# Identity products ahead of the first projections, and the decay tables behind a copy of the first head's queries

## The chip, the cores and the metric

The kernel runs on one core of a Trainium2 chip. A core has a matrix engine (TensorE, PE in the profile), a vector engine (VectorE, DVE), an engine for functions of one argument (ScalarE, ACT), a general engine (GpSimd, POOL) and SyncE (SP), which issues the transfers here. They share an on-chip memory of 128 partitions; TensorE writes into eight banks of PSUM, which VectorE and ScalarE empty. The metric is the device time of one execution, in microseconds, lower being better.

## The reference

The program is a small generator backbone of two layers over 256 latent tokens with a prefix of 256 context tokens, of width 1024. Layer 0 mixes tokens with bidirectional retention in four heads, layer 1 with neighbourhood attention; each is followed by a SwiGLU channel mixer. Every sublayer is modulated by the condition (adaLN; `modulate` is h * (1 + scale) + shift). What matters here is the beginning of layer 0:

```python
cond_lat = jax.nn.silu(c)[:, None, :]
cond_ctx = jax.nn.silu(c_ctx)[None, None, :]
m_lat = jnp.split(cond_lat @ ada_w[i] + ada_b[i], 6, axis=-1)
m_ctx = jnp.split(cond_ctx @ ada_w[i] + ada_b[i], 6, axis=-1)
a_lat = modulate(h_lat, m_lat[0], m_lat[1])
...
q, k, v, g = jnp.split(a @ w_in, [hk, 2 * hk, 2 * hk + hv], axis=-1)
log_gamma = -jnp.exp(decay_param.astype(jnp.float32))
o_ctx, o_lat = bidirectional_scan(ctx_terms, lat_terms)
y = rms_norm(o).transpose(0, 2, 1, 3).reshape(B, n, hv).astype(g.dtype)
return (jax.nn.silu(g) * y) @ w_out
```

The kernel computes the scan as one product of masked scores: for each head, the scores of keys against queries are multiplied by a table of powers of that head's decay and then multiplied with the values.

## The kernel before, in words

Tokens number 512, latents first. Weights arrive from HBM as units of 128 x 1024 floats, in the order of their use. A unit is split into a high half, a rounded copy made by ScalarE (line 124), and a low half, a subtraction on VectorE (line 126); three products (`mm3`, lines 144 to 146) then stand for one product of full precision. A unit takes one of three `raw` buffers while it is loaded and split.

The start of the kernel is a region whose order on every engine is written out by hand (`tc.manual_schedule`). It loads the condition, the adaLN weights and x. `spread_cond` (lines 174 to 184) spreads the context's condition over the partitions: for each of eight columns two products of that column, repeated 128 times, with the identity `identr`; two copies on ScalarE follow. Then a loop runs over eight K tiles of 128 input features. For each, VectorE sums four columns of the modulation (line 229), ScalarE modulates the x of this tile (line 412) and makes its high half (line 417), and TensorE adds the tile's products into eight banks: four of head 0's queries and keys (`qk0_0` to `qk0_3`) and four of its values. The first five K tiles multiply unsplit floats (`whole_products`, lines 355 and 358); for the last three, weights and activations are split (`split_products`, lines 363 to 373, with `low`, line 347, on VectorE). All eight banks are full when the region ends.

Behind the region, the instructions of each engine are put in order when the program is compiled: a planner goes by the order of the program, which is the priority, and by its own estimate of when each instruction would be ready. `tc.issue_after(ins)` adds to this that what is traced in the block stands behind `ins` in the queue of the engine of `ins`; work for other engines is not bound.

`decay_prep` and `decay_table` (lines 441 to 472) make one table for each head, in the order 1, 2, 3, 0. A table takes four exponentials on ScalarE (lines 461 and 466) and three products or sums on GpSimd (lines 462, 463 and 467). One buffer (`Dt`) holds the table; those of heads 1 to 3 are stored to HBM (line 469) and loaded again later, that of head 0 stays. Two scratch tiles of each table use the tag `pf`, which has two buffers. The same tag serves, later in the program, the eight half rows of x that are loaded and scaled into the residual `z` (lines 803 to 810, on GpSimd), and the scores of a head times their table (lines 558 and 562 on VectorE).

`qk_evac` (line 484) empties the banks of queries or keys: VectorE multiplies the latents by the rotary tables (line 492), ScalarE copies the context columns (line 497 from the first bank, line 500 from the second), VectorE combines them, and a split follows (lines 153 and 154). `v_evac` splits the four value banks. After these, TensorE goes on with head 0's gate (`proj_g`, tiles `g`), whose first bank is the one that `qk0_0` leaves, then head 0's scores (`S`), head 1's queries and keys, head 0's values (`O`), and so on.

Of the kernel before, what the change touches and what calls it, by code (L numbers as in the profile page):

```python
# [11 lines left out]
AF = mybir.ActivationFunctionType  # L12
# [6 lines left out]
P = 128  # L19
D = 1024  # L20
KT = D // P
NLAT = 256
# [22 lines left out]
def backbone(ctx: ExitStack, tc: tile.TileContext, wpack, adapack, cond, condcol, xT, xtok, adab, lncol, lnrow,  # L45
             decay, delta, rope, rpb, mask8, out):
    nc = tc.nc
# [31 lines left out]
    def bank(name):  # L79
        return psum.tile([P, 512], F32, tag="bank", name=name)  # L80
# [61 lines left out]
    def mm3(o, s, m, start, stop):  # L142

        nc.tensor.matmul(o, s[0], m[0], start=start, stop=False)  # L144
        nc.tensor.matmul(o, s[0], m[1], start=False, stop=False)  # L145
        nc.tensor.matmul(o, s[1], m[0], start=False, stop=stop)  # L146

    def cut(pair, *idx):
        return pair[0][idx], pair[1][idx]

    def split_into(pair, src, lo_eng=None, src2=None):

        return (nc.scalar.copy(pair[0], src),
                (lo_eng or nc.vector).tensor_tensor(out=pair[1], in0=src, in1=pair[0].bitcast(F32), op=ALU.subtract))
# [19 lines left out]
    def spread_cond():  # L174
        nc.vector.tensor_copy(out=chi, in_=ccol)
        nc.vector.tensor_tensor(out=clo, in0=ccol, in1=chi.bitcast(F32), op=ALU.subtract)
        for half in range(2):
            b = bank(f"cond_{half}")
            for i in range(4):
                k = 4 * half + i  # L180
                for n, c in enumerate((chi, clo)):
                    nc.tensor.matmul(b[:, i * P:i * P + P], c[:, k:k + 1].to_broadcast([P, P]), identr,
                                     start=i == 0 and n == 0, stop=i == 3 and n == 1)
            nc.scalar.copy(condb[1][:, half * 512:half * 512 + 512], b)
# [79 lines left out]
    identr = const.tile([P, P], F32R, name="identr")  # L264
# [56 lines left out]
    with Phase("ret", "yTh", "yTl", "vh", "vl", "kh", "kl") as rp:  # L321
# [12 lines left out]
                                      name=f"adaraw{i}")  # L334
        xts = {}
        lasts = []

        def load_x(kt):
            xts[kt] = rp.tile([P, NTOK], F32, tag=f"yT{'hl'[kt % 2]}{kt // 2 % 2}", name=f"xt{kt}")
            nc.sync.dma_start(xts[kt], xT[kt])  # L340
# [43 lines left out]
            stream.place[16 * RET_H - 4 + i] = (rp, w + "h", w + "l", 1)  # L384
        load_x(0)
        stream.load_to(1)
        spread_cond()
        qk_ps = [bank(f"qk0_{f}") for f in range(4)]
        v_ps = [bank(f"v0_{t}") for t in range(4)]
        for kt in range(KT):  # L390
# [50 lines left out]
        def decay_prep():  # L441
            nc.scalar.activation(lg, lg, AF.Exp)
            nc.gpsimd.tensor_scalar(out=lg, in0=lg, scalar1=-1.0, scalar2=0.0, op0=ALU.mult, op1=ALU.add)
            nc.gpsimd.tensor_scalar(out=lgw[:, 0], in0=lg, scalar1=256.0, scalar2=0.0, op0=ALU.mult, op1=ALU.add)
            nc.gpsimd.tensor_scalar(out=lgw[:, 1], in0=lg, scalar1=-1.0, scalar2=0.0, op0=ALU.mult, op1=ALU.add)
            nc.scalar.activation(dp[0], dlt, AF.Relu)
            nc.scalar.activation(dp[1], dlt, AF.Relu, scale=-1.0)

            nc.gpsimd.memset(dp[2], 1.0)
            nc.gpsimd.affine_select(out=dp[2], in_=dp[2], compare_op=ALU.not_equal, fill=2.0, base=-128,  # L450
                                    pattern=[[1, 384]], channel_multiplier=-1)
# [5 lines left out]
        def decay_table(h):  # L457
            D_ = rp.tile([P, 2, 384], F32, tag="Dt", name=f"Dw{h}")
            e = [rp.tile([P, 384], F32, tag=f"yT{'hl'[i]}3", name=f"de{i}_{h}") for i in range(2)]
            for i in range(2):  # L460
                nc.scalar.activation(e[i], dp[i], AF.Exp, scale=lg[:, 4 * i + h:4 * i + h + 1])
            nc.gpsimd.tensor_tensor(out=e[0], in0=e[0], in1=e[1], op=ALU.mult)
            nc.gpsimd.tensor_tensor(out=D_[:, 1, :], in0=e[0], in1=dp[2], op=ALU.mult)
            x = [rp.tile([P, NTOK], F32, tag="pf", name=f"dx{i}_{h}", bufs=2)[:, 0:384] for i in range(2)]
            for i, rate in enumerate((lg[:, h:h + 1], lgw[:, 1, 4 + h:5 + h])):
                nc.scalar.activation(x[i], dlt, AF.Exp, scale=rate, bias=lgw[:, 0, 4 * i + h:4 * i + h + 1])
            nc.gpsimd.tensor_tensor(out=D_[:, 0, :], in0=x[0], in1=x[1], op=ALU.add)
            if h:
                nc.sync.dma_start(dscr[h], D_)
            else:  # L470
                Dt[h] = D_

        with tc.issue_after(lasts[-1].ins):
            decay_prep()
            for h in (1, 2, 3, 0):
                decay_table(h)

        qk = {}
        vv = {}
        gg = {}  # L480
# [3 lines left out]
        def qk_evac(h, which, ps):  # L484

            f = rp.tile([P, 2, NTOK], F32, tag="qf", name=f"qf{h}{which}", bufs=1)
            scale = 1.0 / 16.0 if which == "q" else 1.0
            m = [rp.tile([P, NLAT], F32, tag=f"rm{i}", name=f"rm{i}_{h}{which}") for i in range(2)]
            x = [f[:, i, 0:NLAT] for i in range(2)]

            def times(o, i, table):
                nc.vector.scalar_tensor_tensor(out=o, in0=ps[i][:, 0:NLAT], scalar=scale, in1=table, op0=ALU.mult,
                                               op1=ALU.mult)

            times(x[0], 0, cosT)
            times(m[1], 0, sinT)
            nc.scalar.activation(f[:, 0, NLAT:], ps[0][:, NLAT:], AF.Copy, scale=scale)  # L497
            times(x[1], 1, cosT)
            times(m[0], 1, sinT)
            nc.scalar.activation(f[:, 1, NLAT:], ps[1][:, NLAT:], AF.Copy, scale=scale)  # L500
            nc.vector.tensor_tensor(out=x[0], in0=x[0], in1=m[0], op=ALU.subtract)
            nc.vector.tensor_tensor(out=x[1], in0=m[1], in1=x[1], op=ALU.add)
            pr = (rp.tile([P, 2, NTOK], F32R, tag=f"{which}h", name=f"{which}h{h}"),
                  rp.tile([P, 2, NTOK], F32R, tag=f"{which}l", name=f"{which}l{h}"))
            split_into(pr, f)
            qk[(h, which)] = pr

        def v_evac(h, ps):
            for t in CTX_FIRST:
                pr = (rp.tile([P, 512], F32R, tag=f"vh{t}", name=f"vh{t}_{h}"),  # L510
                      rp.tile([P, 512], F32R, tag=f"vl{t}", name=f"vl{t}_{h}"))
                split_into(pr, ps[t])
                vv[(h, t)] = pr

        def proj_qk(h):
            for which in "qk":
                ps = []
                for i in range(2):
                    u = stream.next()
                    b = bank(f"{which}{h}_{i}")  # L520
                    for kt in range(KT):
                        mm3(b, cut(u, slice(None), slice(kt * P, kt * P + P)), aT[kt], kt == 0, kt == KT - 1)
                    ps.append(b)
                qk_evac(h, which, ps)
# [12 lines left out]
        def proj_g(h):  # L537
            for i in range(4):
                u = stream.next()
                b = bank(f"g{h}_{i}")  # L540
                for kt in range(KT):
                    mm3(b, cut(u, slice(None), slice(kt * P, kt * P + P)), aT[kt], kt == 0, kt == KT - 1)
                g = rp.tile([P, NTOK], F32, tag=f"g{i}", name=f"g{i}_{h}")
                nc.scalar.activation(g, b, AF.Silu)
                gg[(h, i)] = g
# [254 lines left out]
        for i, w in ((0, "q"), (2, "k")):  # L800
            qk_evac(0, w, qk_ps[i:i + 2])
        v_evac(0, v_ps)
        proj_g(0)
        for t in CTX_FIRST:
            for half in range(2):
# [405 lines left out]
    with Phase("ffn1", "h1h", "h1l") as fp:  # L1211
# [62 lines left out]
        ps = {(t, c): bank(f"e_{t}{c}") for t in range(2) for c, _ in cols[t]}  # L1274
# [138 lines left out]
```

## Time and profile before

| | us |
|---|---|
| median of three runs (lowest, highest) | 1187.77 (1181.21, 1190.56) |
| the profiled execution, its own time | 1184.83 |
| its span, first to last instruction | 1182.8 |
| TensorE busy | 1155.5 (98%) |
| VectorE busy | 786.8 (67%) |
| ScalarE busy | 454.3 (38%) |
| GpSimd busy | 295.5 (25%) |

A line of the profile's timeline gives the start and the length in microseconds, the engine (`PEld` is the loading of TensorE's stationary operand, `SPq` an issue of a transfer), the line of the kernel, the operation, the tile written and the tiles read, and in square brackets the idle time of the engine before it and what ended that. `x8` merges eight instructions. A line of the waits gives who waited for whom, the total, how many times and the longest. A line of the windows gives a stretch and its length, then the busy time and the count of instructions of PE, PEld, DVE, ACT and POOL, the granted clock of TensorE as a share of the full one, the busy share of the transfer engines, and GB/s. A line of a source gives the least, the median and the longest duration in nanoseconds, and the first and last start. Operations that a helper issues all carry the helper's line.

### The profile page before, as it was taken

To read this page: it belongs to the slowest core of one execution; us is meant where nothing else is said; L and a number is where in the kernel's file an instruction comes from. 1 tells how busy PE (TensorE), PEld (TensorE's weight loads), DVE (VectorE), ACT (ScalarE), POOL (GpSimd) and SP (SyncE) were. 2 spreads that over 40 slices of the span, in tenths; PEclk is the share of its full clock that TensorE was granted. 3 is DMA by queue.
4 is the path that set the end of the run, shared out by engine and by line. 5 is a ranking of instruction groups with operands and counts; after the bars stand their busy time and mean duration, and the time that the engine had idled before them with its cause. 6 is when DMAs were issued, how large, how long until landed. Compare 5 with 4: busy or idle time off the path is not lost.

```text
span 1182.8 us, 15310 instructions
## 1 busy us (share of the span) xinstructions
PE 1155.5 (98%) x5670; PEld 961.8 (81%) x5670; DVE 786.8 (67%) x1136; ACT 454.3 (38%) x710; POOL 295.5 (25%) x280
## 2 busy tenths in 40 slices
PE   7999999999999999999999999999999998999997
PEld 5778888888888888888888888887888876888886
DVE  7987956645745589757776476556255577778645
ACT  3482423332333253323122232234355464566530
POOL 0054115104203568000220000025354446200000
PEclk9999999999999999999999999999999999999999
DMA  8756564233434223567456586416588742777650
GB/s 318 277 209 208 163 196 138 90 125 126 137 107 126 88 72 99 186 126 248 178 174 218 160 271 238 149 57 145 154 241 242 198 146 104 233 233 229 210 168 36
DMA packets 70010, 201.72 MB, mean 171 GB/s; under 512 B 14512, under 2 KB 17072, under 8 KB 69936
## 3 DMA queue, kind: packets, MB, share of 16 engines
q1 hardware_dynamic: 69648, 200.23, 53.4%
q8 instruction: 44, 0.72, 0.3%
q10 hardware_dynamic: 288, 0.52, 0.1%
q14 instruction: 30, 0.25, 0.1%
HBM read 187.98 MB, written 2.25 MB: 161 GB/s over the span
## 4 chain that ended last, share of the span: by engine, by line
PE 56%; POOL 2%; DVE 2%; DMA 1%; issue 1%; ACT 0%; DVEq 0%; SPq 0%; POOLq 0%
PE f L145 6%; PE f L146 6%; PE f L144 6%; PE f L855 5%; PE d L145 3%; PE d L146 3%; PE d L144 3%; PE f L856 3%; PE e L145 1%; PE e L144 1%; PE e L146 1%; PE k L144 1%; PE o L1110 1%; PE k L145 1%; PE k L146 1%; PE pT L1097 1%
## 5 line engine op out<-in xcount | busy, mean ns | idle before, releaser
L126 DVE TENSOR_TENSOR wlo<-raw,whi 128x1024 fp32r<-128x1024 f32 x217 | 286.5, 1324 | 209.5 <-ACT whi L124 203.4
L124 ACT CAST whi<-raw 128x1024 fp32r<-128x1024 f32 x220 | 229.7, 1049 | 458.4 <-PE f L145 119.7
L229 DVE CUSTOM_DVE_ANT_0 junk<-adaraw,cond,adab_sb 128x1024 bf16<-128x1024 f32 x160 | 217.4, 1359 | 43.7 <-DMA adaraw<-in_adapack 41.4
L145 PE MATMUL f<-aT,whi 128*128 128x512 f32 (+1 forms) x384 | 143.0, 372 | 2.7 <-DVE aT L760 2.6
L146 PE MATMUL f<-aT,wlo 128*128 128x512 f32 (+1 forms) x384 | 142.5, 371 | 0.0
L144 PE MATMUL f<-aT,whi 128*128 128x512 f32 (+1 forms) x384 | 142.5, 372 | 0.0
L855 PE MATMUL f<-aT,whi 128*128 128x512 f32 x320 | 112.7, 396 | 0.0
L317 POOL TENSOR_TENSOR pb_n<-pa_n,mhalf 128x1 f32<-128x1 f32 x12 | 7.5, 626 | 339.9 <-DVE pa_n L316 339.9
L856 PE MATMUL f<-aT,wlo 128*128 128x256 f32 x320 | 90.1, 282 | 0.5 <-DVE wlo L126 0.4
L145 PEld LDWEIGHTS f<-aT,whi 128*128 128x128 f32 x384 | 72.3, 188 | 15.9 <-DVE aT L760 3.2
L144 PEld LDWEIGHTS f<-aT,whi 128*128 128x128 f32 x384 | 72.2, 188 | 12.6
L146 PEld LDWEIGHTS f<-aT,wlo 128*128 128x128 f32 x384 | 72.3, 188 | 12.4
L855 PEld LDWEIGHTS f<-aT,whi 128*128 128x128 f32 x320 | 60.0, 188 | 14.1
L144 PE MATMUL d<-whi,hh 128*128 128x512 f32 x176 | 68.6, 389 | 0.0
L146 PE MATMUL d<-whi,hl 128*128 128x512 f32 x176 | 68.5, 389 | 0.0
L145 PE MATMUL d<-wlo,hh 128*128 128x512 f32 x176 | 68.5, 389 | 0.0
L146 PE MATMUL v<-whi,aT 128*128 128x512 f32 x160 | 62.5, 392 | 1.8 <-POOL aT L760 1.8
L626 POOL TENSOR_TENSOR z<-t,z 128x512 f32<-128x512 f32 x28 | 44.4, 1595 | 76.3 <-DVE t L624 76.1
L144 PE MATMUL v<-whi,aT 128*128 128x512 f32 x160 | 62.4, 390 | 0.0
L145 PE MATMUL v<-wlo,aT 128*128 128x512 f32 x160 | 62.3, 389 | 0.0
L856 PEld LDWEIGHTS f<-aT,wlo 128*128 128x128 f32 x320 | 60.3, 189 | 1.2 <-DVE wlo L126 1.1
L144 PE MATMUL g<-aT,whi 128*128 128x512 f32 x128 | 50.9, 398 | 2.0 <-ACT qf0q L497 2.0
(287 smaller groups left out, 2444.0 us busy)
## 6 DMA issues: line engine op xcount, KB each, us to landing
raw<-in_wpack SPq DMA_DIRECT2D x228, 512.0 KB, 3.6
adaraw<-in_adapack SPq DMA_DIRECT2D x96, 512.0 KB, 4.5
ln<-in_lnrow SPq DMA_DIRECT2D x16, 256.0 KB, 4.3
braw<-in_rpb SPq DMA_DIRECT2D x8, 512.0 KB, 5.2
kh<-sth SPq DMA_DIRECT2D x32, 128.0 KB, 2.5
kl<-stl SPq DMA_DIRECT2D x32, 128.0 KB, 2.5
gateb<-gscr SPq DMA_DIRECT2D x6, 512.0 KB, 6.1
xt<-in_xT SPq DMA_DIRECT2D x8, 256.0 KB, 4.7
```

The lines of the kernel that those rows point to most:

```text
L124: nc.scalar.copy(hi, raw)
L126: low = eng.tensor_tensor(out=lo, in0=raw, in1=hi.bitcast(F32), op=ALU.subtract)
L144: nc.tensor.matmul(o, s[0], m[0], start=start, stop=False)
L145: nc.tensor.matmul(o, s[0], m[1], start=False, stop=False)
L146: nc.tensor.matmul(o, s[1], m[0], start=False, stop=stop)
L229: nc.vector.tensor_tensor_reduce(out=junk, in0=self.tiles[i], in1=condb[s], scale=1.0, scalar=adab_sb[:, l, m:m + 1], op0=ALU.mult, op1=AL ...
L317: nc.gpsimd.tensor_tensor(out=b, in0=a, in1=mhalf[:, 0:n], op=ALU.pow)
L626: eng.tensor_tensor(out=z[t][:, cs], in0=t2, in1=z[t][:, cs], op=ALU.add)
L855: nc.tensor.matmul(b[i].rearrange("p (a t) -> p a t", a=2), st[0], m, start=kt == 0, stop=False)
L856: nc.tensor.matmul(b[i][:, 0:NLAT], st[1], m[:, 0, :], start=False, stop=kt == KT - 1)
L1097: nc.tensor.transpose(b[:, c:c + P], prob[(hh, qt)][:, kk * P:kk * P + P], ident)
L1110: nc.tensor.matmul(b[hh * 64:hh * 64 + 64, :NLAT], vf[kk][:, c:c + 64], pts[(hh, kk // 2)][:, kk % 2, :], start=kk == 0, stop=kk == 3)
```

## The change

Two things change. Twelve products of the identity with itself are issued on TensorE ahead of `spread_cond`, and fourteen behind it, into a bank that nothing reads. And the block that makes the decay tables moves: it was traced ahead of the first evacuations, with ScalarE's part behind the last high half of the activations (`lasts[-1]`); now it is traced behind the evacuations of head 0's queries, keys and values, with ScalarE's part behind its copy of the second bank of queries (line 500 before).

```diff
+        BUSY = (12, 14)
...
         load_x(0)
         stream.load_to(1)
+
+        idle = bank("idle")
+
+        def busy(n):
+            for i in range(n):
+                nc.tensor.matmul(idle[:, 0:P], identr, identr, start=True, stop=True)
+
+        busy(BUSY[0])
         spread_cond()
+        busy(BUSY[1])
         qk_ps = [bank(f"qk0_{f}") for f in range(4)]
...
-        with tc.issue_after(lasts[-1].ins):
-            decay_prep()
-            for h in (1, 2, 3, 0):
-                decay_table(h)
-
+        evacuated = {}
...
-            nc.scalar.activation(f[:, 1, NLAT:], ps[1][:, NLAT:], AF.Copy, scale=scale)
+            evacuated[(h, which)] = nc.scalar.activation(f[:, 1, NLAT:], ps[1][:, NLAT:], AF.Copy, scale=scale)
...
         for i, w in ((0, "q"), (2, "k")):
             qk_evac(0, w, qk_ps[i:i + 2])
         v_evac(0, v_ps)
+        with tc.issue_after(evacuated[(0, "q")].ins):
+            decay_prep()
+            for h in (1, 2, 3, 0):
+                decay_table(h)
         proj_g(0)
```

## The prediction

> **What bounds the kernel now.** I read the page first, then TensorE's waits over the whole span.
>
> ```profile
> span 1182.8 us, 15310 instructions
> PE 1155.5 (98%) x5670; PEld 961.8 (81%) x5670; DVE 786.8 (67%) x1136; ACT 454.3 (38%) x710; POOL 295.5 (25%) x280
> PE T L782 <- DVE z L714: 2.7, 1, 2.7
> PE g L144 <- ACT qf0q L497: 2.0, 1, 2.0
> PE qk L355 <- ACT am L412: 1.4, 1, 1.4
> ```
>
> TensorE is in work for 98% of the span, so a microsecond counts only if TensorE's own row moves. Two of its waits lie where the diff works: 1.4 us ahead of the first product with x and 2.0 us ahead of head 0's gate. Busy does not say how fast, so I asked for the granted clock in quarter microseconds around the second wait, and in whole ones behind the 2.7 us wait.
>
> ```profile
> 66.50:66.75 0.25, 0.25 (x2) 0.21 (x1) 0.25 (x1) 0.25 (x1) 0.00 (x0) 0.50 1.11 426
> 69.75:70.00 0.25, 0.25 (x2) 0.21 (x1) 0.25 (x2) 0.25 (x1) 0.25 (x1) 0.76 1.06 410
> 983.00:984.00 1.00, 0.89 (x5) 0.30 (x2) 0.91 (x4) 0.93 (x3) 0.00 (x0) 1.00 0.92 360
> ```
>
> The column behind POOL's is the clock: halved from about 66.4 to 69.8, after a wait of 2.0 us, and full after one of 2.7 us. So a wait does not always cost the clock. At the start the column reads 1.00 throughout, but the timeline shows otherwise:
>
> ```profile
> 2.10 0.29 POOL L265 CAST identr<-ident 128x128 fp32r<-128x128 f32 x1
> 5.51 0.41 PE L182 MATMUL cond<-identr,clo 128*128 128x128 f32 x1
> 8.50 0.41 PE L182 MATMUL cond<-identr,clo 128*128 128x128 f32 x1
> 10.35 3.78 PE L355 MATMUL qk<-am,raw 128*128 128x256 f32 x8 [1.44 <-ACT am L412]
> 16.31 1.89 PE L355 MATMUL qk<-am,raw 128*128 128x256 f32 x8
> 19.75 1.89 PE L355 MATMUL qk<-am,raw 128*128 128x256 f32 x8
> ```
>
> Eight passes take 3.78 us in the first half of the first K tile and 1.89 in the second: the first products run at half clock. Half a K tile takes 19.75 - 16.31 = 3.44 us at full speed and took 16.31 - 10.35 = 5.96 here: 2.5 us lost.
>
> **Part one: the products on the identity.** The identity is there at 2.39 us (2.10 + 0.29). The condition's 14 steps from 5.51 to 8.50 are 2.99/14 = 0.214 us each. Twelve more at that rate, an estimate, end at 2.4 + 2.6 = 5.0, before the condition's products could start anyway: no cost. Fourteen behind 8.7 end at 11.7 if the clock stays halved, at 10.2 if it is full by then; the first real product starts at 10.35. Cost: 0 to 1.35 us, of half-clock work. I take 0, since TensorE is then busy without a gap from 2.4 on, while before it was idle until 5.2 and again for 1.4 us. The gain at the second half is the 2.5 us above. How much of it lives to the end of the region:
>
> ```profile
> SPq L110 <- PE v L358: 21.8, 4, 6.6
> 41.30 1.28 DVE L229 CUSTOM_DVE_ANT_0 junk<-adaraw,cond,adab_sb 128x1024 bf16<-128x1024 f32 x1 [0.75 <-DMA adaraw<-in_adapack]
> 52.78 1.07 PE L370 MATMUL qk<-aT,whi 128*128 128x512 f32 x4
> 53.24 0.68 DVE L347 TENSOR_TENSOR aT<-am,aT 128x512 fp32r<-128x512 f32 x1
> 54.60 0.39 PE L372 MATMUL qk<-aT,whi 128*128 128x512 f32 x1
> ```
>
> Weight loads wait for TensorE to free their buffers (21.8 us in the first 66), and the adaLN weights queue behind them, so with TensorE ahead VectorE's 0.75 us wait should go too. But K tile 6 has its low half from VectorE at 53.24 + 0.68 = 53.92, or 53.17 without that wait. TensorE wants it at 54.60, with the gain at 52.1. So VectorE is late next: the gain is 54.60 - 53.17 = **1.4 us** (0.7 if the loads do not come earlier). K tile 7 keeps that distance.
>
> A word on what wakes the clock: the 16 condition products filled 5.3 to 8.7 us and the clock was still half at 10.35; it was full by 16.31. The Trainium skill ("TensorE: Matmul & The Clock Gate", What's actually happening) says that a busy window of about 3.4 us, free-running, releases it. By that rule 9 us of identity products suffice, and the sum stays as it is; the trace shows no release by products of 128 columns alone, which is the second rival below.
>
> **Part two: the end of the region.**
>
> ```profile
> 55.20 1.28 ACT L442 ACT_TABLE_LOAD   x1
> 60.26 0.39 PE L373 MATMUL qk<-aT,wlo 128*128 128x512 f32 x1
> 60.72 0.39 PE L373 MATMUL qk<-aT,wlo 128*128 128x512 f32 x1
> 60.89 3.82 DVE L126 TENSOR_TENSOR wlo<-raw,whi 128x1024 fp32r<-128x1024 f32 x2 [1.08 <-ACT whi L124]
> 63.44 0.39 PE L373 MATMUL v<-whi,aT 128*128 128x512 f32 x1
> 64.97 0.41 DVE L492 SCALAR_TENSOR_TENSOR rm_0q<-qk,sinT 128x256 f32<-128x256 f32 x1
> 65.41 0.38 ACT L497 ACTIVATE qf0q<-qk 128x256 f32<-128x256 f32 x1
> 65.85 0.50 PE L144 MATMUL g<-aT,whi 128*128 128x512 f32 x1 [2.02 <-ACT qf0q L497]
> 66.42 0.58 PE L146 MATMUL g<-aT,wlo 128*128 128x512 f32 x1
> 69.79 0.43 PE L145 MATMUL g<-aT,whi 128*128 128x512 f32 x1
> L126 DVE TENSOR_TENSOR wlo<-raw,whi 128x1024 fp32r<-128x1024 f32 x217 | 286.5, 1324 | 209.5 <-ACT whi L124 203.4
> L124 ACT CAST whi<-raw x4: 1028/1036/1043, 53.6 to 63.4; 128x1024 fp32r<-128x1024 f32 x4
> ```
>
> All eight banks are full at the end of the region (63.44 + 0.39 = 63.83); the gate waits for the first query bank, complete since 60.65 (60.26 + 0.39). Its readers came late: ScalarE's copy at 65.41, behind the tables, and VectorE's at 64.97, behind two splits that took 3.82 us where one takes 1.32 on average over the kernel. The tables' products on GpSimd ran beside them. With the tables behind the copies both causes go. The **2.0 us** wait goes (1.6 would stay, 65.38 - 63.83, if only ScalarE were cured), and the half clock with it: from 66.42 to 69.79 stand 8 steps, 3.37 us, against some 0.23 each in 60.26 to 60.72 (two steps, 0.46), so 3.37 - 1.84 = **1.5 us**. Together with part one TensorE reaches head 0's gate work 1.4 + 2.0 + 1.5 = 4.9 us earlier.
>
> A rule of the Trainium skill speaks against the 1.5 (the same page, Why this matters for your kernels): only gaps over about 3 us lose the clock; by it that term is 0, and the first rival below would give 1.5 us less. The rows above measure a loss behind 2.02 us, so the trace decides.
>
> **Part three: what the tables were early for.** ScalarE began them at 55.20. Now nothing of them can start before the second query bank is copied: complete at 60.72 + 0.39 - 1.4 = 59.7, then two copies of 0.38 give 60.5, or 62.5 if the two weight casts that wait there (1.04 each) stay ahead. Later by 5.3 to 7.3 us; I take 6. Behind the tables hangs a chain:
>
> ```profile
> 63.65 0.33 SPq L469 DMA_DIRECT2D dscr<-Dw  x1
> 66.97 1.06 POOL L467 TENSOR_TENSOR Dw<-dx,dx 128x384 f32<-128x384 f32 x1 [3.35 <-DMA dscr<-Dw]
> L467 POOL TENSOR_TENSOR Dw<-dx,dx x4: 1057/1594/1999, 59.5 to 83.3; 128x384 f32<-128x384 f32 x4
> L463 POOL TENSOR_TENSOR Dw<-de,dp x4: 1073/1479/2001, 61.7 to 81.4; 128x384 f32<-128x384 f32 x4
> 103.10 1.25 POOL L810 TENSOR_SCALAR z<-xr 128x512 f32<-128x512 f32 x2 [2.44 <-DMA xr<-in_xtok]
> 103.75 1.33 DVE L558 TENSOR_TENSOR pf<-S,Dw 128x512 f32<-128x512 f32 x2 [4.16 <-POOL z L810]
> 110.67 2.30 POOL L154 TENSOR_TENSOR pl<-pf,ph 128x256 fp32r<-128x256 f32 x2 [1.94 <-ACT ph L153]
> 117.04 0.28 PE L144 MATMUL O<-ph,vh 128*128 128x256 f32 x1
> ```
>
> One table buffer serves four tables, so each waits for the store of the last (3.35 us here). The tables' scratch tiles share two buffers with the rows of x, eight transfers that go through GpSimd two at a time, and head 0's scores take the same two buffers after those: VectorE waits 4.16 us for the last rows and starts at 103.75. The last low half is done at 110.67 + 2.30 = 112.97, and TensorE uses that tile at 117.04. So the slack is 4.1 us. The tables 6 us later and TensorE 4.9 us earlier make 10.9: TensorE would wait 10.9 - 4.1 = 6.8 us in head 0's values. What can shrink the chain: GpSimd's eight writes of the tables sum to about 4 x 1.59 + 4 x 1.48 = 12.3 us, at their shortest 4 x 1.06 + 4 x 1.07 = 8.5. So 0 to 3.8 us; I take 2, about the middle: VectorE and GpSimd will overlap there less, but not never. Wait: **4.8 us**, then up to 1.5 us of half clock again (the 2.0 us wait had it, the 2.7 us wait did not): I take **0.8**.
>
> ScalarE gets more changes of function table (each 1.28 us, as at 55.20), since the gate's SiLU now falls between exponentials. Its 38% of the span hides that; the cost, if the cover is gone, is already in the 5.3 to 7.3. The queue of loads (SP) waits at each store of a table with weight loads behind; those weights are split long before use, so I put it at nothing, or at what the chain already has.
>
> **Sum** against the profiled execution (1184.83 us with a span of 1182.8; the runs shown have the median 1187.77, 2.9 above it, and spread over 9.4): -1.4 - 2.0 - 1.5 + 4.8 + 0.8 = +0.7. The gain is handed back 50 us later. On the profiled execution 1185.5, on the median **1188.5 us**.
>
> **The rivals.** *The gain stays* (for: the planner can put the next value projection's products ahead of the values if it sees the late tables, or the chain shrink by all of the 6.8; against: TensorE's order follows the program there now, and the real 4.16 us wait shows that its estimate of this chain was short). Then -4.9: 1182.9. Chance 0.30.
> *The products do not wake the clock* (slower). For: the 16 condition products did not. Then fourteen of them end at 11.7 and push the half-clock start by 1.35 us, 0.7 at full speed; the region ends 0.7 later instead of 1.4 earlier, so do the copies, the tables and the end of the wait: +0.7 + 2.1 = +2.8, 1190.6. It decides if the clock is still half when the first product with x starts. Against: an unbroken 8 us of work has no counterpart in the trace. Chance 0.15.
> *The end of the region stays as it is*, the copy being prompt but VectorE's splits still first: the 1.6 us wait and the 1.5 stay, TensorE arrives 1.8 us early, not 4.9. Since the late chain sets the end of the wait, the result is again about +0.7. Chance 0.10. The forecast itself keeps 0.45.
>
> **Range and chances.** Fast end: the gain stays, less what the spread of the runs allows a median (about 3): 1180. Slow end: a chain 7.3 later, nothing shrunk, and the clock lost: -4.9 + 8.1 + 1.5 = +4.7, with some 3 for the spread: 1195.5. Within 1% (11.9 us, about what a measurement of this kernel tells from no change) lie all four cases; only a re-planned order elsewhere reaches beyond. Faster by over 1%: 0.04, within: 0.91, slower: 0.05.
>
> **What would show it.** Right: passes of 0.24 us (1.89/8) from the first product with x; no wait ahead of the gate and no halved clock near 66; a wait of TensorE for GpSimd's low halves in head 0's values, with the scores' product on VectorE starting near 108. Wrong: the first eight passes still taking 3.78 us; no wait in the values (the first rival, some 1183); or tables that start before 60 us.

## The result, and the profile after

The changed kernel takes 1194.77 us in the median (1193.91 to 1196.47), the kernel before beside it 1186.25. The ratio is 1.0076, with a 95% interval of 1.0058 to 1.0095. So the change costs about 8.5 us, where the forecast had +0.7. It lies inside the range that was given, 0.7 us from its slow end, and within the 1% that was called no change, but the interval excludes no change, and the sum was wrong by some 8 us.

The profiled execution of the kernel after took 1194.17 us with a span of 1192.4, 9.6 us more than the span before. The page's head, then some of TensorE's waits over the whole span:

```profile
span 1192.4 us, 15363 instructions
PE 1166.1 (98%) x5696; PEld 971.4 (81%) x5696; DVE 785.5 (66%) x1136; ACT 458.1 (38%) x712; POOL 295.4 (25%) x280
```

```profile
PE T L788 <- DVE z L720: 2.7, 1, 2.7
PE O L144 <- ACT ph L153: 2.5, 1, 2.5
PE g L144 <- DVE vl L154: 2.3, 1, 2.3
PE O L145 <- POOL pl L154: 1.7, 2, 1.0
```

TensorE's busy time grew by 10.6 us (1166.1 - 1155.5). The identity products are 6.0 of them (2.82 + 3.19 in the next view); the rest, 4.6 us, must be the kernel's own work done more slowly, since its products are the same. The wait ahead of head 0's gate is still there, with another releaser, and two lines of waits in head 0's values (`O`) are new. I follow the span from its start, in the timeline of TensorE. Lines 356, 359 and 393 after are 355, 358 before and the identity products.

```profile
2.44 2.82 PE L393 MATMUL idle<-identr 128*128 128x128 f32 x12 [2.44 <-POOL identr L265]
9.13 3.19 PE L393 MATMUL idle<-identr 128*128 128x128 f32 x14
12.11 3.66 PE L356 MATMUL qk<-am,raw 128*128 128x256 f32 x8
...
17.33 1.89 PE L356 MATMUL qk<-am,raw 128*128 128x256 f32 x8
```

From 2.44 on TensorE works but for 0.4 us ahead of the condition's products, yet the first eight passes with x take 3.66 us, as they did before (3.78), and start 1.76 us later (12.11 against 10.35). More than nine microseconds of work did not wake the clock. The second half of the K tile stands at 17.33, before at 16.31: one microsecond late. What happens at the end of the region, in the timeline of TensorE, VectorE and ScalarE:

```profile
62.66 2.49 DVE L126 TENSOR_TENSOR wlo<-raw,whi 128x1024 fp32r<-128x1024 f32 x2 [0.57 <-ACT whi L124]
63.80 2.04 ACT L153 CAST vh<-v 128x512 fp32r<-128x512 f32 x4
65.07 0.42 DVE L498 SCALAR_TENSOR_TENSOR qf0q<-qk,cosT 128x256 f32<-128x256 f32 x1
65.71 1.08 ACT L124 CAST whi<-raw 128x1024 fp32r<-128x1024 f32 x1
66.40 1.88 DVE L154 TENSOR_TENSOR vl<-v,vh 128x512 fp32r<-128x512 f32 x3
66.66 0.42 ACT L503 ACTIVATE qf0q<-qk 128x256 f32<-128x256 f32 x1
66.93 0.41 ACT L506 ACTIVATE qf0q<-qk 128x256 f32<-128x256 f32 x1
67.14 0.50 PE L144 MATMUL g<-aT,whi 128*128 128x512 f32 x1 [2.28 <-DVE vl L154]
67.36 1.28 ACT L452 ACT_TABLE_LOAD   x1
```

The tables have left ScalarE's queue here, but ScalarE did not take the copies of the queries next. Four casts of value banks and a cast of weights stand ahead of them, and the first copy comes at 66.66, later than before (65.41). VectorE again had two splits of weights ahead of its first rotary product (62.66, then 65.07). The gate waits 2.28 us instead of 2.02, and the profile names VectorE's low halves of the values (`vl`). The first of the three ends at 67.08 (0.68 us from 66.40), 0.06 us ahead of the gate. ScalarE's first copy ends at 67.08 too, so this profile alone does not tell which of them the gate waits for; a run below does. Taken from the gate's start, the region ended at 67.14 - 2.28 = 64.86, against 63.83 before. The function table that begins the decay tables is loaded at 67.36, 12.2 us later than before (55.20). Head 0's values, further on:

```profile
110.55 0.69 DVE L564 TENSOR_TENSOR pf<-S,Dw 128x512 f32<-128x512 f32 x1 [5.59 <-POOL z L820]
114.99 0.39 PE L144 MATMUL O<-ph,vh 128*128 128x512 f32 x1
119.35 0.38 PE L144 MATMUL O<-ph,vh 128*128 128x256 f32 x1 [2.53 <-ACT ph L153]
120.35 0.38 PE L145 MATMUL O<-pl,vh 128*128 128x256 f32 x1 [0.62 <-POOL pl L154]
120.63 1.33 POOL L154 TENSOR_TENSOR pl<-pf,ph 128x256 fp32r<-128x256 f32 x1 [0.33 <-ACT ph L153]
122.01 0.58 PE L145 MATMUL O<-pl,vh 128*128 128x256 f32 x1 [1.03 <-POOL pl L154]
131.45 0.40 PE L144 MATMUL v<-whi,aT 128*128 128x512 f32 x1
```

Here is the chain of the forecast: the rows of x on GpSimd, then the scores' product on VectorE at 110.55 (103.75 before), the high and low halves, and TensorE waiting for them three times, 2.53 + 0.62 + 1.03 = 4.2 us: 2.53 for a high half of ScalarE, 1.65 for low halves of GpSimd. Then the clock, in windows of half a microsecond (the clock is the column behind POOL's):

```profile
121.00:121.50 0.50, 0.00 (x0) 0.00 (x0) 0.50 (x2) 0.50 (x1) 0.50 (x1) 0.91 0.08 31
121.50:122.00 0.50, 0.00 (x0) 0.00 (x0) 0.50 (x1) 0.00 (x0) 0.46 (x1) 0.50 0.00 0
...
128.00:128.50 0.50, 0.50 (x3) 0.36 (x3) 0.50 (x2) 0.00 (x0) 0.00 (x0) 0.77 0.00 0
```

It is halved from about 121.4 to 128.2, 6.8 us, which loses 3.4. The first products of head 1's values start at 131.45; before they started at 123.70:

```profile
123.70 0.40 PE L144 MATMUL v<-whi,aT 128*128 128x512 f32 x1
```

So 7.75 of the 9.6 us are lost by here.

### The profile page after: what moved, and what is told of

It reads as the page before. It is cut to its first block, busy times and chain, and to the rows that moved or that the text cites. A ratio compares the mean times of both kernels' runs of the same rounds, so it can differ in the third digit from the quotient of the medians.

```text
span 1192.4 us, 15363 instructions
## 1 busy us (share of the span) xinstructions
PE 1166.1 (98%) x5696; PEld 971.4 (81%) x5696; DVE 785.5 (66%) x1136; ACT 458.1 (38%) x712; POOL 295.4 (25%) x280
## 4 chain that ended last, share of the span: by engine, by line
PE 58%; DVE 2%; POOL 1%; issue 0%; DMA 0%; ACT 0%; DVEq 0%; SPq 0%; POOLq 0%
PE f L145 6%; PE f L146 6%; PE f L144 6%; PE f L865 6%; PE d L144 3%; PE d L145 3%; PE d L146 3%; PE f L866 3%; PE e L145 1%; PE e L144 1%; PE e L146 1%; PE k L144 1%; PE o L1120 1%; PE k L145 1%; PE k L146 1%; PE v L146 1%
```

## The experiments

The theory, after the result: the identity products do not wake the clock and cost little; the tables' move makes the loss, through the two buffers of the tag `pf`, and through the clock that the wait costs. Each run below that was executed several times has the ratio of its median to the kernel before, timed beside it.

**The tables' move alone.** The changed kernel without the identity products.

```diff
-        busy(BUSY[0])
         spread_cond()
-        busy(BUSY[1])
```

> The tables moved, no identity products. My theory: the wait of TensorE in head 0's values comes from the late chain of tables, rows of x and scores, and not from the identity products. Then the region ends as before (63.8 us), the first row of the values stands still for some 4 to 5 us as after the change (4.2), half clock follows it, and the time is 1 us less than after the change (which starts its first real product 1.76 us later): 1193.5. Rival: the identity products are what made the kernel slower; then this one is at or under the time of before, 1182 to 1186.

Measured: 1196.14 us, ratio 1.0072 (1.0047 to 1.0097). Its waits, and the start of head 1's values:

```profile
PE O L144 <- ACT ph L153: 2.5, 1, 2.5
PE O L145 <- POOL pl L154: 2.1, 3, 1.1
130.38 0.40 PE L144 MATMUL v<-whi,aT 128*128 128x512 f32 x1
```

The move alone gives the whole loss. The time is above the 1193.5 that was expected, but the kernel before beside it also stood higher, at 1188.13 instead of 1186.25. Head 1's values start 1.07 us earlier than in the changed kernel (130.38 against 131.45), as expected.

**The identity products alone.** The kernel before with the twelve and fourteen products.

```diff
+        busy(12)
         spread_cond()
+        busy(14)
```

> The identity products, with the tables where they were before. My theory: they do not wake the clock and only push the first products with x back, so the region ends 1.0 us later than before (64.9 against 63.8) and so does all that follows, with no wait in head 0's values: 1187, +0.1% on 1186.25. Rival: the products make the loss: 1192 or more. Other rival: they help once the tables are out of the way: the first eight passes take 1.9 us, and the time is 1184 or less.

Measured: 1187.74 us, ratio 0.9993 (0.9974 to 1.0013). The products make no difference that this comparison, good to about 2 us, can see. In the trace the region ends at 64.38 (66.57 - 2.19), 0.55 us later than in the profile before, where 1.0 was expected; their price where no wait hides it comes in the last pair below.

**The rows of x behind head 0's values.** The changed kernel, but the eight half rows of x, which share the two `pf` buffers with the tables' scratch and the scores, are loaded and scaled after head 0's values are issued instead of before.

```diff
         proj_g(0)
-        for t in CTX_FIRST:
-            for half in range(2):
+        def load_rows():
+            for t in CTX_FIRST:
+                for half in range(2):
...
             values(h)
+            if h == 0:
+                load_rows()
```

> The changed kernel, with the loading and scaling of the rows of x moved behind head 0's values in the program, so that they no longer stand between the tables and the scores in the two shared buffers. My theory: the wait in the values is made by that chain, some 14 to 18 us long; it goes, with the half clock behind it: 4.2 + 3.4 = 7.6 us less than after the change, 1187. Rival: the tables themselves are too late (the last is done at 96 us) or ScalarE's backlog holds the halves of the scores: then a wait of 2 us or more stays and the time is over 1190.

Measured: 1188.05 us, ratio 0.9999 (0.9980 to 1.0017). The timeline of the gate, ScalarE's first copy, the last low half of the scores and the values:

```profile
66.27 0.50 PE L144 MATMUL g<-aT,whi 128*128 128x512 f32 x1 [2.04 <-DVE vl L154]
66.37 0.38 ACT L503 ACTIVATE qf0q<-qk 128x256 f32<-128x256 f32 x1
104.35 0.74 POOL L154 TENSOR_TENSOR pl<-pf,ph 128x256 fp32r<-128x256 f32 x1 [0.28 <-ACT ph L153]
114.14 0.39 PE L144 MATMUL O<-ph,vh 128*128 128x512 f32 x1
122.51 0.40 PE L144 MATMUL v<-whi,aT 128*128 128x512 f32 x1
```

The last low half starts at 104.35 instead of 120.63, there is no wait in the values, and the loss is gone, with the tables as late as in the changed kernel. So the late tables hurt only through the rows of x that queue behind them. The edit moves the rows' transfers and their work on GpSimd along with their claim to the buffers; that the two buffers are the link rests on VectorE's wait of 5.59 us for `z` in the profile after, since the scores' product reads and writes nothing else that the rows touch. A buffer of their own for the rows was not tried. The gate's wait is untouched: the loss did not come from there.

The trace also tells what the gate waits for. It starts at 66.27, before ScalarE's first copy of the queries (66.37), and 0.06 us behind the first low half of the values (65.53 + 0.68 = 66.21). The run of the tables' move alone shows the same: that low half ends at 65.10, the gate starts at 65.16 and the copy at 65.29. So with the tables moved the gate waits no longer for the copy but for VectorE, where splits of weights and four rotary products stand ahead of that low half. That the gate's first bank is then one that the values leave is my reading; the profile does not name banks.

**The rows of x later, without the change.** The same edit on the kernel before.

```diff
             values(h)
+            if h == 0:
+                load_rows()
```

> The kernel before with the rows of x behind head 0's values and nothing else. There was no wait in the values, so cutting the chain should give nothing: values of head 1 near 123.7, 1184 to 1189. If it is over 4 us faster, the chain did more in the kernel before than I thought.

One timed execution, 1192.45 us, above the 1184 to 1189 expected. There is no gain in the trace, as expected: the gate waits 2.2 us and head 1's values start at 123.45, against 123.70. Its time is high by stretches at half clock in places that the edit doesn't touch, as these windows of its profile show, where the kernel before had 1.00:

```profile
800.00:810.00 10.00, 8.19 (x28) 5.42 (x27) 7.57 (x11) 5.03 (x11) 6.12 (x6) 0.83 0.86 86
990.00:1010.00 20.00, 18.11 (x73) 13.89 (x72) 11.65 (x29) 12.27 (x31) 11.40 (x17) 0.83 0.31 104
```

Before the change the chain had 4.1 us to spare, and freeing it earlier buys nothing. One execution cannot price an edit here; the trace can place it.

**Wider identity products.** The kernel before with twelve products of the identity with four copies of itself, 512 columns each, ahead of `spread_cond` and none behind. The copies are made by GpSimd; the bank is one that nobody reads.

```diff
+        wide = aT2[7].rearrange("p a t -> p (a t)")[:, 0:512]
+        for i in range(4):
+            nc.gpsimd.tensor_copy(out=wide[:, i * P:i * P + P], in_=ident)
+        for i in range(12):
+            nc.tensor.matmul(idle, identr, wide, start=True, stop=True)
         spread_cond()
```

> The kernel before with twelve identity products of 512 columns (four identities side by side) ahead of the condition's products, none behind; tables as before. What is asked is only which products wake the clock. Theory one: a product of 128 columns keeps the array at work for half of its 0.214 us, the other half being the load of the stationary operand, and that is not enough; products of 512 columns wake it after some 3.4 to 6.8 us, so that the condition's products, or at the latest the first products with x, run at full pace (0.107 us, or 0.24 us a pass). Theory two: operands that are nearly all zeros do not wake it; then the first eight passes with x still take some 3.7 us. The condition comes some 3 us later than before, so the whole time may rise by 1 to 3 us.

One timed execution, 1192.83 us, 4.7 above the median of the kernel before (1188.13) where 1 to 3 were expected. The copies came late behind other work of GpSimd, so the products did too, and a wait of 6.2 us ahead of the gate spoils the time. The question was the clock:

```profile
7.42 4.41 PE L395 MATMUL idle<-aT,identr 128*128 128x512 f32 x12 [7.42 <-POOL aT L391]
11.73 0.28 PE L182 MATMUL cond<-identr,clo 128*128 128x128 f32 x1
13.29 0.27 PE L182 MATMUL cond<-identr,clo 128*128 128x128 f32 x1
14.74 2.00 PE L356 MATMUL qk<-am,raw 128*128 128x256 f32 x8 [1.17 <-ACT am L424]
```

The 14 steps of the condition's products from 11.73 to 13.29 are 0.111 us each, where they were 0.214, and the first passes with x take 2.00 us, not 3.78. Products on the same sparse identity wake the clock when they are wide.

**The copies first.** The changed kernel, with VectorE's rotary products and ScalarE's copies of head 0's queries held ahead of the other evacuations and of the gate's work (the block `first` stands around `proj_g` too), so that the order at the gate is the one that the prediction took for granted.

```diff
+        stream.split_to(stream.used + 1)
+        qk_evac(0, "q", qk_ps[0:2])
+        first = [tc.issue_after(i[(0, "q")].ins) for i in (evacuated, rotated)]
+        for f in first:
+            f.__enter__()
+        qk_evac(0, "k", qk_ps[2:4])
         v_evac(0, v_ps)
+        for f in reversed(first):
+            f.__exit__(None, None, None)
...
```

> The changed kernel (products and moved tables), with head 0's query copies on ScalarE and the rotary products on VectorE put ahead of the weight splits and of the value and key evacuations: all of these stand behind them in their queues, but for the first gate unit's split. My theory: the gate wait (2.28 us) is made by that order, not by the tables, so it goes or falls under 0.5 us; the tables start at about 63 instead of 67.4, some 4.4 earlier, so the last halves of head 0's scores come that much earlier too, while TensorE comes 2 us earlier; the wait in the values shrinks from 4.2 to some 2 us, and the time falls by 4 to 5 us against the change: 1190 to 1191. Rival: the gate wait stays at 2 us because another bank or a late weight unit takes its place; then the time stays at 1194 or more.

Measured: 1194.46 us, ratio 1.0056 (1.0038 to 1.0074); the expectation of 1190 to 1191 missed. The wait at the gate is gone, and the copies come at 61.73 and 62.40. But:

```profile
62.80 1.28 ACT L452 ACT_TABLE_LOAD   x1
65.50 2.94 ACT L124 CAST whi<-raw 128x1024 fp32r<-128x1024 f32 x3
69.78 0.62 ACT L471 ACTIVATE de<-dp,lg 128x384 f32<-128x384 f32 x1
118.26 2.08 PE L144 MATMUL O<-ph,vh 128*128 128x512 f32 x4 [6.50 <-ACT ph L153]
```

The table load comes 4.6 us earlier (62.80), but ScalarE's queue puts casts between it and the first exponential at 69.78, so the tables themselves gain nothing; TensorE, freed of the gate's wait, arrives early and stands 6.5 us in front of the values instead of 4.2. What the gate gives is handed back at the values.

**Copies first and rows later, without identity products.** The kernel of the run above, without its identity products and with the rows of x behind head 0's values.

```diff
-        busy(BUSY[0])
         spread_cond()
-        busy(BUSY[1])
...
             values(h)
+            if h == 0:
+                load_rows()
```

> No identity products; the tables behind the copy of the queries as in the change; the query copies ahead in both queues as in the run before it; and the rows of x behind head 0's values. My theory: no wait ahead of the gate and none in the values, so head 1's values begin near 120.5 (123.7 before), some 3 us earlier: 1185 against 1188, -0.25%. Rival: what TensorE gains is lost again at a later wait, as at 430 or 980 us, or in half clock there: 1188, no change.

Measured: 1183.14 us, ratio 0.9958 (0.9941 to 0.9975), faster than both kernels. TensorE waits neither at the gate nor in the values:

```profile
63.75 0.39 PE L144 MATMUL g<-aT,whi 128*128 128x512 f32 x1
...
119.86 0.40 PE L144 MATMUL v<-whi,aT 128*128 128x512 f32 x1
```

Head 1's values start 3.8 us earlier than before (119.86 against 123.70): 2.1 at the gate (63.75 against 65.85) and 1.7 behind it. The forecast's 2.0 and 1.5 us at the gate do exist, once the copies really go first and the chain is taken off the two buffers. Against the kernel timed beside it (1188.63) the median gains 5.5 us; what it has beyond the 3.8 of the trace, and beyond the 3 us expected, was not placed.

**Narrow and wide products where no wait hides them.** On this kernel, once the change's products, and once ten ahead of the condition and four behind that read the same identity four times over as 512 columns, so that they start as early as the narrow ones.

```diff
+        busy(10)
         spread_cond()
+        busy(4)
...
+nc.tensor.matmul(idle.rearrange("p (a b) -> p a b", b=P), identr,
+                 identr.unsqueeze(1).to_broadcast([P, 4, P]), start=True, stop=True)
```

> The kernel with tables and copies moved and the rows of x behind head 0's values, which had no wait left ahead of the gate or in the values, plus the change's twelve and fourteen identity products of 128 columns. Theory (products of 128 columns do not wake the clock and push the first products with x by 1.0 us): first product with x near 12.1 us, first eight passes 3.7 us, region end near 64.9 instead of 63.9, and, as no wait is left to swallow it, about 1.0 us slower than without the products: 1184. Rival (they cost nothing even here, because weights or VectorE are late at K tile 6 anyway): 1183.1.

> The same, but the identity products (ten ahead of the condition's, four behind) read the identity four times over as 512 columns, from the same tile at the same time as the change's. They are written to a bank that nobody reads. Theory (the width decides): ten products of 0.43 us from 2.4 us on wake the clock by about 6, the condition's products take 0.11 us each, the first product with x starts near 10.3 and its eight passes take 1.9 us, not 3.8; TensorE is 2.0 us earlier at the second K tile, of which 1.4 lasts to the end of the region: 1181.7. Rival (the sparse identity keeps the clock low at any width): first passes 3.8 us, 1183 to 1184. Other rival (the gain at the start is lost again because VectorE or the weights are late at K tile 6): passes awake, region end as without products, 1183.1.

Measured beside one another: narrow 1185.01 us, ratio 0.9975 (0.9956 to 0.9995); wide 1182.58 us, ratio 0.9956 (0.9938 to 0.9974). Narrow first, then wide:

```profile
11.97 3.44 PE L355 MATMUL qk<-am,raw 128*128 128x256 f32 x8
64.89 0.39 PE L144 MATMUL g<-aT,whi 128*128 128x512 f32 x1
```

```profile
2.45 4.63 PE L391 MATMUL idle<-identr 128*128 128x512 f32 x10 [2.45 <-POOL identr L265]
8.39 0.27 PE L182 MATMUL cond<-identr,chi 128*128 128x128 f32 x1
8.50 0.27 PE L182 MATMUL cond<-identr,clo 128*128 128x128 f32 x1
10.62 1.99 PE L355 MATMUL qk<-am,raw 128*128 128x256 f32 x8 [0.20 <-ACT am L421]
62.55 0.39 PE L144 MATMUL g<-aT,whi 128*128 128x512 f32 x1
PE qk L372 <- DVE aT L347: 0.7, 1, 0.7
```

Both are about 1 us above the times expected (1184 and 1181.7). The only difference between the two is the width and number of the products. The narrow ones leave the clock asleep and bring the gate at 64.89, 1.1 us later than without any (63.75). The wide ones wake it by 8.4 (steps of 0.11 us from 8.39 on), the first passes take 1.99 us, and the gate starts at 62.55, 1.2 us earlier. The medians are 2.4 us apart and the traces 2.34. The wide pattern costs no copies, since the identity is read four times. Beside the kernel without products (1183.14, ratio 0.9958) the wide one's ratio is the same, so the 1.2 us rest on the trace and on the difference from the narrow one.

## Where the prediction was right and where it was wrong

The terms of its sum, measured in the two profiled executions:

| term | forecast, us | measured, us |
|---|---|---|
| start, up to the end of the region | -1.4 | +1.0 (64.86 - 63.83) |
| wait ahead of the gate | -2.0 | +0.3 (2.28 - 2.02) |
| half clock behind that wait | -1.5 | -1.5 (1.5 before, none in this profile) |
| waits in head 0's values | +4.8 | +4.2 |
| half clock behind them | +0.8 | +3.4 |
| sum | +0.7 | +7.4 (7.75 at head 1's values) |

The time lies in the range by luck rather than by the sum: the range's slow end was made of a chain that does not shrink, a lost clock and 3 us for the spread of the runs, with the whole gain of 4.9 us still in it.

**The start failed at "I take 0, since TensorE is then busy without a gap".** That is the second rival's mechanism: the products don't wake the clock, the first passes stay at half speed, and the region ends 1.0 us later (the rival had 0.7). The trace before held the warning, sixteen condition products that left the clock asleep; I gave them too little weight (0.15) because unbroken work had no counterpart there. The term itself was right for products that do wake the clock: with 512 columns the region ended 1.2 us earlier, and VectorE was late next, as said: TensorE waits 0.7 us for its low half (line 347).

**The gate failed at "with the tables behind the copies both causes go".** Taking work from in front of an instruction does not bring it to the front: ScalarE took value casts and a weight cast before the copies, and VectorE kept its two splits. The wait that stayed is VectorE's: it ends with the first low half of the values, which stands behind these splits and the rotary products. So the third rival, a gate that stays as it is for VectorE's splits, had the nearer mechanism, though it took the copy to be prompt. With the queries held first on both engines, the gate's wait did go. The 1.5 us behind the wait came by luck: the wait stayed, and this time the clock was not lost behind it.

**The chain was right, with errors that cancelled.** The place of the new wait and its size (4.8 against 4.2) were as forecast; of its releasers the forecast named GpSimd's low halves (1.65 us) and not ScalarE's high half (2.53). The rows of x behind the late tables were its cause: the run with the rows later shows it. But its inputs were off. The slack was read off the use of the last high half (117.04); the low half is used at 117.16, so it was 4.2 us and not 4.1. The tables started 12.2 us later instead of 6, since the casts went ahead of the copies; TensorE reached the values only 0.3 us earlier (114.99 against 115.33) instead of 4.9; the chain from the table load to the end of the last low half shrank by 3.2 us (from 57.8 to 54.6) instead of 2. With these the forecast's own formula gives 12.2 + 0.3 - 4.1 - 3.2 = 5.2 us, 1.0 more than measured.

**The half clock was mis-sized.** I took 0.8 behind the new wait, half of what the gate's had cost. In this profile it was 3.4, from a halved stretch of 6.8 us that begins in the last of three waits in a row. The runs point the same way: span times one minus the mean granted clock, the time lost to it by the column, averages 6.8 us in the 25 runs of the kernel before that were timed beside the first experiments, and 11.6 in the seven of the change. The 4.8 between them are not a share of the 8.5 us, since the column also counts half clock in which TensorE has no work: in the profile after, TensorE's last product ends at 1184.4, and the clock is halved from 1186.4 to the end of the span, 3 us by this measure. The run of the tables' move alone loses 11.7, that of the rows later 6.1, as the kernel before: without the waits in the values the extra loss is gone. The rule of the Trainium skill that the prediction weighed ("TensorE: Matmul & The Clock Gate", Why this matters for your kernels: gaps of about 3 us lose the clock) would have given none behind waits of 2.53, 0.62 and 1.03 us; the windows above measure it.

What remains of the profiled difference, 9.6 - 7.75 = 1.9 us, lies far behind head 1's values. The products of `v` near 800 us start 7.72 us late (805.20 against 797.48), so nothing was lost or gained for 670 us; the products of `T` start 9.0 late (991.15 against 982.15), and the end is 9.6 late. In between the profile after has halved stretches that the profile before has not, at 810 to 820 and 990 to 1010 (mean clock 0.83 in both). By the column they lose 5.1 us, by the starts of TensorE's work 1.9. The kernel before with the rows of x later has like ones at 800 to 810 and 990 to 1010, so I don't put them down to the change. Whether the wait in the values makes later ones likelier was not tested.

## What to carry to other kernels

Work that is moved out of the way of a critical instruction leaves room for whatever else is ready: look at the queue behind it, and hold the critical instruction first if it is to gain, and read off the trace whether the wait is still for that instruction. Follow each moved step through the buffers that it shares, down to the last user of the tag; here a late table delayed rows of the residual, and those the scores. To wake TensorE's clock ahead of real work, use wide products (512 columns here, not 128), and read the durations of the first real ones, not the busy time.

## What the hardware showed

The clock is not woken by busy time alone. In the change TensorE was in products of 128 columns from 2.44 to 12.1 us (twelve, the condition's sixteen, and fourteen), at some 0.21 us a step (the last fourteen in 12.11 - 9.13 = 2.98 us), with one gap of 0.4 us, and stayed at half speed. With ten products of 512 columns from 2.45 on, the steps halved by 8.39, after 5.9 us (the last 1.4 in the condition's narrow products); with twelve from 7.42 on, the condition's steps took 0.11 us by 11.73, within 4.3 us. The Trainium skill ("TensorE: Matmul & The Clock Gate", What's actually happening) has the clock released by some 3.4 us of sustained work and calls it a matter of time, not of the number of products; the runs here differ: 9.7 us of narrow products did not release it. Each product has its own load of the stationary operand, wide or narrow (ten loads for the ten wide ones in the profile), so a load for each is not the difference. An estimate: the ten wide steps take 4.43 us at half speed (2.45 to 6.88), 0.44 each, so a quarter of the columns would take 0.11, about half of the narrow step of 0.21. That the array idles in the other half, while the operand is loaded, is the likely reason; it was not measured by itself.

A wait of about 2 us costs the clock in one execution and not in the next: 2.02 us ahead of the gate did in the profile before, 2.28 did not in the profile after. The wait of 2.7 us at `T`, which both kernels have, did not in the profile before and did in the profile after, where it ends at 991.15:

```profile
993.00:994.00 1.00, 1.00 (x4) 0.80 (x3) 0.93 (x4) 0.97 (x4) 0.55 (x1) 0.50 0.30 107
```

By the column, the time lost to it differs between executions of the same kernel by several microseconds (1.2 to 11.9 in those of the kernel before). In this kernel that is the size of most edits: a wait of TensorE is to be priced with the clock's chance, and a small edit by several executions or by its place in the trace.

In the profile after, the granted clock's column reads 1.00 over the first 12 us, while a step of 128 columns takes 0.21 us, about twice the 0.11 of the runs with wide products:

```profile
0.00:12.00 12.00, 9.17 (x42) 8.98 (x42) 4.91 (x9) 4.11 (x6) 2.71 (x15) 1.00 0.83 303
```

At the cold start of these runs only the durations of the products tell.
